# A two-layer hybrid encoder on one core: where the value products, the low halves and the gate products are issued

## The chip, the core and the metric

One core of a Trainium2 chip runs the whole program. TensorE (PE) multiplies, with its own queue for loading weights (PEld); VectorE (DVE), ScalarE (ACT) and GpSimd (POOL) work element by element; SyncE (SP) issues nearly all DMAs. The metric is the device time of one execution in microseconds; lower is better.

## The reference

Two layers over 512 tokens of a prompt and 256 of a sample, 1024 features, fp32. The same weights serve both.

```
h = rmsnorm(x, norm_mix_g);  proj = h @ w_in
qa, ka, va, qb, kb, vb, rb, glf, glb, ga, gb = split(proj)
ya = mixer_a(qa, ka, va) @ w_branch_a      # windowed softmax attention, 3 dilations x 8 heads
yb = mixer_b(qb, kb, vb, rb, ...) @ w_branch_b   # gated linear attention (GLA), both directions
x = x + (sigmoid(ga) * ya + sigmoid(gb) * yb) @ w_out
h = rmsnorm(x, norm_ffn_g)
x = x + relu(h @ w_ff1)**2 @ w_ff2
```

After the second layer comes one more rmsnorm. The changed code concerns the 1536 columns of `va`, taken in six blocks of 256 that are called values 0 to 5 (block 4 has the 32 low-rank columns `glf`, `glb` of the GLA decay beside it), the gates `ga` and `gb`, and the last stores.

## The kernel before, in words

Every fp32 product is made of three passes of a faster fp32 format: a factor is split into a high half (`whi`, `hh`, `sph`) by a cast on ACT and a low half (`wlo`, `hl`, `spl2`) by a subtraction on DVE or POOL, and hi x hi, hi x lo and lo x hi are added in PSUM. Dense products take their accumulators from a PSUM pool of three banks (`acc`): a fourth tile can start only when the first has been read out. A tile over the 1024 features is 8 x 3 = 24 matmuls.

The program is written as a stream of dense products beside steps of other work. `add` puts a product into the stream, `dense_piece` issues the next eighth or so of a tile, `weave(steps, total)` issues the steps with dense pieces spread evenly among them, up to `total` microseconds of an inner estimate, and `run_dense` issues what is left of the stream. The framework's scheduler then fixes each engine's order. An engine runs its own order strictly, and waits where an operand or a buffer is not ready.

A layer goes like this. **First stage**: `values(i, ...)` for three of six blocks: weights are loaded and split by `wunit` (`wlo` on the engine that `side[0]` names), six tiles of 128 tokens are multiplied, ACT and DVE split each result (`vst`) and SP stores it to `v_dram`; in between, the steps `lower` and `upper` (L1175 on) prepare operands of the Strassen form, normalised `xT`, their sums `t` and low halves `ql`, mostly on DVE. In layer 0 the prompt's tokens are loaded and their norm's statistics made in the middle of it (`statistics()`). **Projections** for queries and keys (`long_dense`). **Attention rounds**: one round before the first pair of heads, then `p` = 0, 1, 2, 3; PE, DVE and ACT work on scores, exponentials and outputs, and dense work is woven in as filler: the other values, gates `gate_a` and GLA values. **GLA heads**. **Gates and branches**: `gate_b(k)` multiplies two half-token tiles of 384 columns, which ACT evacuates into `sgb`; `split_from` loads the mixer's output from `ma_dram`, adds two parts on DVE, and splits the sum (`spl` on DVE, `sph` on ACT) into `xa`, which the product with `w_branch_a` reads. Then the product with `w_out`, the FFN, and in layer 1 `to_tokens`, which transposes the result and stores it in twelve DMAs.

Where the rows below say L235 they mean the matmuls of all ordinary dense products; L434 is a product of the projections, L173 the cast and L120 the subtraction of a split, L621 the gate's evacuation, L631 the cast in `split_from`, L626 its loads.

Of the kernel before, what the change touches and what calls it, by code (L numbers as in the profile page):

```python
# [24 lines left out]
NK = DM // 128  # L25
# [51 lines left out]
def encoder(ctx: ExitStack, tc: tile.TileContext, a, y_prompt, y_sample):  # L77
    nc = tc.nc
# [54 lines left out]
    def constants():  # L133
        nc.sync.dma_start(out=gmix[:, 1, :], in_=a["norm_mix_g"][1].rearrange("(k p) -> p k", p=128))
        for l in range(DEPTH):
            nc.sync.dma_start(out=gffn[:, l, :], in_=a["norm_ffn_g"][l].rearrange("(k p) -> p k", p=128))
        nc.sync.dma_start(out=qsc, in_=a["qscale"])
        nc.sync.dma_start(out=gfin, in_=a["final_norm_g"].rearrange("(k p) -> p k", p=128))
# [19 lines left out]
    ma_dram = drm.tile([2, 512, T], F32, name="ma_dram")  # L158
# [4 lines left out]
    side = [nc.gpsimd]  # L163
# [58 lines left out]
    def weave(steps, total):  # L222
        done = 0.0
        for i, step in enumerate(steps):
            step()
            while done < total * (i + 1) / len(steps):
                t = dense_piece()
                if t is None:
                    break
                done += t  # L230
# [392 lines left out]
    def split_from(drams, k, alloc_hi, alloc_lo):  # L623
        xs = [b3("spl") for _ in drams]
        for x, dram in zip(xs, drams):
            nc.sync.dma_start(out=x, in_=dram[k * 128:(k + 1) * 128, :])  # L626
        x = xs[0]
        for y in xs[1:]:
            nc.vector.tensor_tensor(x, x, y, op=ALU.add)
        hi, lo = alloc_hi("sph", F32R), alloc_lo("spl2", F32R)  # L630
        nc.scalar.copy(hi, x)  # L631
        sub(lo, x, hi)
        return hi, lo
# [398 lines left out]
    class Last:  # L1032
# [19 lines left out]

        def to_tokens(self, m):
            last = len(self.y) == NT and not any(self.left)
            if last:
                r = self.rms()
            for b in range(NT):
                if b not in self.y:
                    self.y[b] = b3("ya", shape=(128, 2, 384))
                y = self.y[b]  # L1060
                tp = pm("tp", (128, 2, 128))
                for i in range(2):
                    nc.tensor.transpose(tp[:, i, :], self.xT[m + 4 * i][:, b * 128:(b + 1) * 128], ident)
                if not last:
                    dst = y[:, :, m * 128:(m + 1) * 128]
                    nc.vector.tensor_copy(dst, tp) if (m + b) % 2 else nc.scalar.copy(dst, tp)
                    continue
                rb = r[:, b:b + 1]
                z = b3("yb", shape=(128, 2, 128))
                nc.scalar.activation(z, tp, AF.Copy, scale=rb)  # L1070
                nc.vector.tensor_scalar(y, y, rb, None, op0=ALU.mult)
                out, row = (y_prompt, b) if b < 4 else (y_sample, b - 4)
                out = out.rearrange("o s d -> (o s) d")[row * 128:(row + 1) * 128].rearrange("t (i c) -> t i c", i=2)
                nc.sync.dma_start(out=out[:, :, 0:384], in_=y)
                nc.sync.dma_start(out=out[:, :, 384:512], in_=z)

        def rms(self):
            sp = pm("st", (128, NT))
# [28 lines left out]
    def spill(k, xT):  # L1107
        nc.sync.dma_start(out=x_dram[k * 128:(k + 1) * 128, :], in_=xT[k])
# [4 lines left out]
    for l in range(DEPTH):  # L1113
        w_in = a["w_in"][l]
        nm = norm
        gxs = []
        side[0] = nc.gpsimd

        def values(i, low_rank, x, scaled, order=tuple(range(NT))):

# [34 lines left out]
            tok_dense(parts, nco, x, evac, order)  # L1155


        for i, low_rank in ((0, False), (4, True), (2, False)) if l == 0 else ((4, True), (2, False), (0, False)):
            values(i, low_rank, nm.h, True, (4, 5, 0, 1, 2, 3) if l == 0 else tuple(range(NT)))
        prefetch()  # L1160
        if l == 0:
            statistics = load_x(a["x_prompt"].rearrange("o s d -> (o s) d"), 0, SEQ, norm)
            for _ in range(2 * NK):
                dense_piece()
            statistics()
            for k in range(NK):
                spill(k, xT)
            constants()

        ops = Quads(4)  # L1170
# [13 lines left out]
        steps = [lambda: [nm.ready(t0, n) for t0, n in nm.parts]]  # L1184
# [10 lines left out]
            units.append([(c0 + hd * 128, R_GLA + 4 * i + hd, None if i else 128.0 ** -0.5, False)  # L1195
                          for i, c0 in enumerate((C_QB, C_KB))])
        long_dense(w_in, [(u[0][0], u[1][0]) for u in units], ops, projections([[c[1:] for c in u] for u in units]))
        weave(steps, 40 if l else 30)
        side[0] = nc.vector
        while len(stream) > 7 * len(units):  # L1200
            dense_piece()

# [48 lines left out]
        steps = [lambda b=b: gate_transpose(b) for b in range(NT)]  # L1251
# [49 lines left out]
            steps += [f] + nothing  # L1301
        steps += singles + [combine] + nothing * 4
        q, k, following = attention_load(1, x3)
        values(1, False, h_at, False)
        weave(steps + following, 14)
        run_dense()
        for p in range(4):
            steps = []
            if p < 3:
                scores, singles, combine, values1, loads, finish1 = attention_steps(p + 1, q, k)  # L1310
                extra = {4: scores[0], 6: scores[1], 8: scores[2], 15: loads[1]}
                extra.update({9 + i: f for i, f in enumerate(singles)})
                extra[11] = lambda f=extra[11], g=loads[0]: (f(), g())
            else:
                extra = {}
            for i, stages in enumerate(values_of):
                steps += stages
                if i in extra:
                    steps.append(extra[i])
            steps.append(finish)  # L1320
            if p < 3:
                steps += [combine] + nothing * 6
                values_of, finish = values1, finish1
            if p < 2:
                q, k, following = attention_load(p + 2, x3)
                steps += following
            if p == 0:
                values(3, False, h_at, False)
                values(5, False, h_at, False)
            elif p < 3:  # L1330
                for j in ((0, 1, 2), (3, 4))[p - 1]:
                    gate_a(j, True)
            else:
                gd = gla_dense(0, w_in, h_at, gn)
            weave(steps, (32, 23, 15, 32)[p])
            run_dense()

        def fetch_gates():
# [25 lines left out]
        def gate_b(k):  # L1364
            def evac(ci, t0, n, acc):
                if t0 == 0:
                    sgb.append(f3("sgb"))
                ins = gate(sgb[k][:, t0:t0 + n], acc[:, :n])
                if k == NK - 1 and t0:
                    with tc.issue_after(ins.ins if hasattr(ins, "ins") else ins):  # L1370
                        nc.scalar.preload_act_table_set("natural_log_exp_and_others")

            feat_dense(w_in, C_GB + k * 128, h_at, evac, splits=HALVES)

        xa = [split_from((ma_dram[0], ma_dram[1]), j, f3, f3) for j in range(4)]
        for j in range(4):
            gate_b(j)

        def evac(k, t0, n, acc):
            s = ta[k][:, t0:t0 + n]  # L1380
# [127 lines left out]
```

## Time and profile before

| | |
|---|---|
| runs | 3019.0, 3027.43, 3030.77 us, median 3027.43 |
| profiled execution | 3024.05 us, of which its span is 3022.2 us; mean granted clock 0.986 |
| PE | busy 2909.2 us, 96% |
| DVE | 2162.5 us, 72% |
| ACT | 1451.5 us, 48% |
| POOL | 64.7 us, 2% |

The span is from the first to the last instruction of the profiled execution. Busy time of engines overlaps, so the shares don't add up; an engine with 96% still hides stalls of some microseconds each and matmuls that run at half the clock.

### The profile page before, as it was taken

How to read it: one execution, taken by the hardware profiler on the slowest of the kernel's cores; microseconds unless marked ns; L12 is line 12 of the kernel's file. 1: busy time of each engine (PE TensorE's matmuls, PEld its weight loads, DVE VectorE, ACT ScalarE, POOL GpSimd, SP SyncE). 2: the span in 40 equal slices, each digit the busy share in tenths (PEclk: the TensorE clock that was granted, in tenths of full speed). 3: DMA queues.
4: the chain of work that ended last, by engine and by line, in shares of the span. 5: the costliest groups of instructions: out<-in, count | busy, mean ns of one | idle time of the engine just before them, and what ended most of it. 6: DMA issues, size and time to landing. Idle time of an engine off the chain costs nothing.

```text
span 3022.2 us, 49144 instructions
## 1 busy us (share of the span) xinstructions
PE 2909.2 (96%) x18428; PEld 2825.7 (93%) x18428; DVE 2162.5 (72%) x4594; ACT 1451.5 (48%) x3110; POOL 64.7 (2%) x128
## 2 busy tenths in 40 slices
PE   7999999999899999999999999899989999999997
PEld 7999988999799999999889999889988899999997
DVE  7767577887448777676986676778763587777767
ACT  5454677556234433333445547775552253333334
POOL 2000000000000000000010000000000000000000
PEclk9999999999999999999999999999999999999998
DMA  6345655233332222222234456643242231222212
GB/s 200 126 136 178 204 163 148 85 99 107 115 94 84 63 70 67 59 68 68 90 130 148 144 162 211 172 118 102 71 149 94 67 94 57 70 58 76 70 57 70
DMA packets 415070, 328.09 MB, mean 109 GB/s; under 512 B 44240, under 2 KB 369264, under 8 KB 414832
## 3 DMA queue, kind: packets, MB, share of 16 engines
q1 hardware_dynamic: 414832, 324.94, 35.3%
q8 instruction: 146, 2.39, 0.3%
q14 instruction: 92, 0.75, 0.1%
HBM read 248.44 MB, written 76.43 MB: 107 GB/s over the span
## 4 chain that ended last, share of the span: by engine, by line
PE 80%; DVE 8%; DMA 4%; ACT 3%; issue 1%; SPq 1%; POOL 0%; DVEq 0%; ACTq 0%
PE acc L235 41%; PE wA L434 11%; PE wA L360 8%; PE wC L434 5%; PE wC L360 4%; PE wB L434 3%; PE wB L360 2%; PE go L984 1%; DMA v_dram<-vst 1%; PE op L782 1%; DVE mt L799 1%; PE pt L770 1%; DVE xT L1462 1%; PE cp L906 1%; PE up L962 1%
## 5 line engine op out<-in xcount | busy, mean ns | idle before, releaser
L235 PE MATMUL acc<-hh,whi 128*128 128x384 f32 x1024 | 345.7, 338 | 0.0
L235 PE MATMUL acc<-hh,wlo 128*128 128x384 f32 x1024 | 344.2, 336 | 0.0
L235 PE MATMUL acc<-hl,whi 128*128 128x384 f32 x1024 | 343.7, 336 | 0.0
L173 ACT CAST whi<-raw 128x1024 fp32r<-128x1024 f32 (+1 forms) x176 | 185.2, 1053 | 291.7 <-PE acc L235 184.3
L120 DVE TENSOR_TENSOR wlo<-raw,whi 128x1024 fp32r<-128x1024 f32 x164 | 200.5, 1222 | 107.2 <-ACT whi L173 98.3
L434 PE MATMUL wA<-qh,aop 128*128 128x384 f32 x960 | 262.4, 339 | 4.3 <-ACT u L478 3.5
L1447 DVE SCALAR_TENSOR_TENSOR rl<-acc,nr 128x384 f32<-128x384 f32 x128 | 71.1, 555 | 190.6 <-PE acc L235 189.3
L235 PEld LDWEIGHTS acc<-hl,whi 128*128 128x128 f32 x1024 | 192.1, 188 | 0.9 <-DVE hl L549 0.4
L235 PEld LDWEIGHTS acc<-hh,whi 128*128 128x128 f32 x1024 | 192.2, 188 | 0.3
L235 PEld LDWEIGHTS acc<-hh,wlo 128*128 128x128 f32 x1024 | 192.2, 188 | 0.3
L434 PEld LDWEIGHTS wA<-qh,aop 128*128 128x128 f32 x960 | 176.8, 190 | 6.0 <-ACT u L478 4.1
L434 PE MATMUL wC<-qh,aop 128*128 128x384 f32 x640 | 178.3, 337 | 0.9 <-ACT aop L284 0.7
L434 PE MATMUL wA<-ql,aop 128*128 128x384 f32 x480 | 162.6, 339 | 0.0
L235 PE MATMUL acc<-whi,qh 128*128 128x256 f32 x528 | 155.2, 294 | 0.9 <-ACT whi L173 0.9
L235 PE MATMUL acc<-wlo,qh 128*128 128x256 f32 x528 | 151.5, 287 | 1.4 <-DVE wlo L120 1.4
L235 PE MATMUL acc<-whi,ql 128*128 128x256 f32 x528 | 150.6, 285 | 0.0
L1462 DVE TENSOR_TENSOR xT<-xT,wA 128x384 f32<-128x384 f32 x256 | 135.1, 548 | 16.6 <-PE wA L360 16.3
L284 ACT CAST sh<-s 128x512 fp32r<-128x512 f32 x128 | 78.1, 619 | 141.6 <-DVE s L334 100.6
L1448 ACT ACTIVATE hq<-rl 128x384 f32<-128x384 f32 x128 | 67.0, 524 | 153.5 <-DVE rl L1447 153.5
L284 ACT CAST aop<-raw 128x512 fp32r<-128x512 f32 x120 | 73.8, 619 | 120.4 <-PE wA L434 47.1
L235 PE MATMUL acc<-spl,whi 128*128 128x256 f32 (+1 forms) x384 | 129.9, 338 | 0.0
L284 ACT CAST aop<-wr 128x512 fp32r<-128x512 f32 x120 | 74.2, 619 | 115.6 <-PE wA L434 63.2
(355 smaller groups left out, 9109.5 us busy)
## 6 DMA issues: line engine op xcount, KB each, us to landing
raw<-in_w_in SPq DMA_DIRECT2D x88, 512.0 KB, 3.8
raw<-in_w_ff SPq DMA_DIRECT2D x64, 512.0 KB, 4.1
p_dram<-o SPq DMA_DIRECT2D x64, 384.0 KB, 2.3
v_dram<-vst SPq DMA_DIRECT2D x72, 256.0 KB, 2.2
raw<-in_w_in SPq DMA_DIRECT2D x64, 256.0 KB, 3.3
wr<-in_w_in SPq DMA_DIRECT2D x64, 256.0 KB, 4.6
raw<-in_w_ff SPq DMA_DIRECT2D x64, 256.0 KB, 3.4
raw<-in_w_ff SPq DMA_DIRECT2D x128, 128.0 KB, 2.8
```

The costliest lines, as they stand in the source:

```text
L120: eng.tensor_tensor(out, x, hi.bitcast(F32), op=ALU.subtract)
L173: nc.scalar.copy(hi, raw)
L235: nc.tensor.matmul(acc[:, :n], wt, xt, start=(k == 0 and j == 0), stop=(k == nkt - 1 and j == 2))
L284: nc.scalar.copy(hi, x)
L360: nc.tensor.matmul(acc[:, :HT], x, y, start=(new and p == 0 and j == 0), stop=(p == quads.n - 1 and j == 2), skip_group_check=True)
L434: nc.tensor.matmul(acc[:, :HT], x, y, start=(new and p == 0 and j == 0), stop=(p == n - 1 and j == 2), skip_group_check=True)
L770: nc.tensor.transpose(pt[:, g, hh, :], pr[hh][:, g * 128:(g + 1) * 128], ident)
L782: nc.tensor.matmul(op[:, hh], v[:, hh].rearrange("p s c -> p (s c)"), pT[g][:, hh].rearrange("p s c -> p (s c)"), start=(g == 0), stop=(g ...
L799: nc.vector.tensor_tensor(dst, dst, src, op=ALU.add)
L1447: nc.vector.scalar_tensor_tensor(r, acc[:, :n], 0.0, fnorm.r[:, t0:t0 + n], op0=ALU.max, op1=ALU.mult)
L1448: nc.scalar.activation(q[0][:, t0:t0 + n], r, AF.Square)
L1462: nc.vector.tensor_tensor(x, x, acc, op=ALU.add)
```

## The change

Four edits. (1) `values(1)` moves from the round before the first pair into the first stage; `values(3)` takes its place, `gate_a(0)` moves from round 1 to round 0 in place of `values(3)`, and the totals of the weaves follow. (2) POOL makes the low halves of weights only up to the prompt's statistics of layer 0; from then on DVE does. Before, POOL made them in the first stage of both layers. (3) The four products `gate_b(0)` to `gate_b(3)` are put into the stream, and 24 pieces of it issued, before the four `split_from` of `xa`. (4) The smaller one of each two last stores is issued from ACT's queue after the loop.

```diff
--- before.py
+++ after.py
@@ -1052,6 +1052,7 @@
 
         def to_tokens(self, m):
             last = len(self.y) == NT and not any(self.left)
+            stores = []
             if last:
                 r = self.rms()
             for b in range(NT):
@@ -1072,7 +1073,9 @@
                 out, row = (y_prompt, b) if b < 4 else (y_sample, b - 4)
                 out = out.rearrange("o s d -> (o s) d")[row * 128:(row + 1) * 128].rearrange("t (i c) -> t i c", i=2)
                 nc.sync.dma_start(out=out[:, :, 0:384], in_=y)
-                nc.sync.dma_start(out=out[:, :, 384:512], in_=z)
+                stores.append((out[:, :, 384:512], z))
+            for out, z in stores:
+                nc.scalar.dma_start(out=out, in_=z)
 
         def rms(self):
             sp = pm("st", (128, NT))
@@ -1114,7 +1117,6 @@
         w_in = a["w_in"][l]
         nm = norm
         gxs = []
-        side[0] = nc.gpsimd
 
         def values(i, low_rank, x, scaled, order=tuple(range(NT))):
 
@@ -1155,7 +1157,7 @@
             tok_dense(parts, nco, x, evac, order)
 
 
-        for i, low_rank in ((0, False), (4, True), (2, False)) if l == 0 else ((4, True), (2, False), (0, False)):
+        for i, low_rank in ((0, False), (4, True), (2, False), (1, False)) if l == 0 else ((4, True), (2, False), (0, False), (1, False)):
             values(i, low_rank, nm.h, True, (4, 5, 0, 1, 2, 3) if l == 0 else tuple(range(NT)))
         prefetch()
         if l == 0:
@@ -1165,6 +1167,7 @@
             statistics()
             for k in range(NK):
                 spill(k, xT)
+            side[0] = nc.vector
             constants()
 
         ops = Quads(4)
@@ -1195,8 +1198,7 @@
             units.append([(c0 + hd * 128, R_GLA + 4 * i + hd, None if i else 128.0 ** -0.5, False)
                           for i, c0 in enumerate((C_QB, C_KB))])
         long_dense(w_in, [(u[0][0], u[1][0]) for u in units], ops, projections([[c[1:] for c in u] for u in units]))
-        weave(steps, 40 if l else 30)
-        side[0] = nc.vector
+        weave(steps, 56 if l else 44)
         while len(stream) > 7 * len(units):
             dense_piece()
 
@@ -1301,7 +1303,7 @@
             steps += [f] + nothing
         steps += singles + [combine] + nothing * 4
         q, k, following = attention_load(1, x3)
-        values(1, False, h_at, False)
+        values(3, False, h_at, False)
         weave(steps + following, 14)
         run_dense()
         for p in range(4):
@@ -1325,14 +1327,14 @@
                 q, k, following = attention_load(p + 2, x3)
                 steps += following
             if p == 0:
-                values(3, False, h_at, False)
                 values(5, False, h_at, False)
+                gate_a(0, True)
             elif p < 3:
-                for j in ((0, 1, 2), (3, 4))[p - 1]:
+                for j in ((1, 2), (3, 4))[p - 1]:
                     gate_a(j, True)
             else:
                 gd = gla_dense(0, w_in, h_at, gn)
-            weave(steps, (32, 23, 15, 32)[p])
+            weave(steps, (23, 15, 15, 32)[p])
             run_dense()
 
         def fetch_gates():
@@ -1372,9 +1374,11 @@
 
             feat_dense(w_in, C_GB + k * 128, h_at, evac, splits=HALVES)
 
-        xa = [split_from((ma_dram[0], ma_dram[1]), j, f3, f3) for j in range(4)]
         for j in range(4):
             gate_b(j)
+        for _ in range(3 * NK):
+            dense_piece()
+        xa = [split_from((ma_dram[0], ma_dram[1]), j, f3, f3) for j in range(4)]
 
         def evac(k, t0, n, acc):
             s = ta[k][:, t0:t0 + n]
```

ACT's order in layer 0 around the gates; `whi` is the high half of a gate's weights, `mbt` the end of the GLA part, `sph` the four casts of `split_from`, `sgb` the gates' evacuations. Before:

```order
L1017 COPY mbt_9081<-tp_9650 128x256
L1017 COPY mbt_9081<-tp_9671 128x256
L1017 COPY mbt_9081<-tp_9681 128x256
L631 CAST sph_9713<-spl_9708 128x768
L631 CAST sph_9722<-spl_9717 128x768
L631 CAST sph_9731<-spl_9726 128x768
L631 CAST sph_9740<-spl_9735 128x768
L621 ACTIVATE sgb_9781<-acc_9756 128x384
L621 ACTIVATE sgb_9781<-acc_9783 128x384
L621 ACTIVATE sgb_9840<-acc_9815 128x384
L173 CAST whi_9929<-raw_9927 128x1024
L621 ACTIVATE sgb_9840<-acc_9842 128x384
```

After:

```order
L621 ACTIVATE sgb_9745<-acc_9720 128x384
L1017 COPY mbt_9081<-tp_9671 128x256
L1017 COPY mbt_9081<-tp_9681 128x256
L621 ACTIVATE sgb_9745<-acc_9747 128x384
L621 ACTIVATE sgb_9804<-acc_9779 128x384
L631 CAST sph_9811<-spl_9806 128x768
L173 CAST whi_9929<-raw_9927 128x1024
L621 ACTIVATE sgb_9804<-acc_9842 128x384
L631 CAST sph_9820<-spl_9815 128x768
L631 CAST sph_9829<-spl_9824 128x768
L631 CAST sph_9838<-spl_9833 128x768
L621 ACTIVATE sgb_9899<-acc_9874 128x384
```

Three evacuations moved ahead of the first cast, a fourth between the first and the second, and the fifth stands behind the fourth cast.

POOL's order from the start of the program's weights on (its `wlo` of layer 0, then the zeroing of attention buffers); before:

```order
L120 TENSOR_TENSOR wlo_203<-raw_200,whi_202 128x1024
L120 TENSOR_TENSOR wlo_209<-raw_206,whi_208 128x1024
L120 TENSOR_TENSOR wlo_296<-raw_292,whi_295 128x1152
L120 TENSOR_TENSOR wlo_559<-raw_555,whi_558 128x1152
L120 TENSOR_TENSOR wlo_565<-raw_562,whi_564 128x1024
L120 TENSOR_TENSOR wlo_847<-raw_844,whi_846 128x1024
L663 MEMSET qk_3157 64x768
```

After:

```order
L120 TENSOR_TENSOR wlo_203<-raw_200,whi_202 128x1024
L120 TENSOR_TENSOR wlo_209<-raw_206,whi_208 128x1024
L120 TENSOR_TENSOR wlo_296<-raw_292,whi_295 128x1152
L663 MEMSET qk_3333 64x768
L663 MEMSET qk_3334 64x768
```

DVE's order in the first stage of layer 0, after the change, where two of these three subtractions now stand (behind line 1055 the changed file's line numbers are up to four higher):

```order
L318 TENSOR_TENSOR t24_528<-xT_104,t24_528 128x384
L1140 SCALAR_TENSOR_TENSOR vst_548<-acc_504,rt_180,vst_548 128x4x64
L120 TENSOR_TENSOR wlo_556<-raw_552,whi_555 128x1152
L120 TENSOR_TENSOR ql_542<-t24_528,qh_541 128x768
L120 TENSOR_TENSOR wlo_562<-raw_559,whi_561 128x1024
L1155 CAST gx_594<-eye_79 128x2
L1140 SCALAR_TENSOR_TENSOR vst_590<-acc_565,rt_180,vst_590 128x4x64
L1150 TENSOR_SCALAR gl_595<-acc_565,rt_180 128x32
```

The subtractions `wlo_556` and `wlo_562` stand between the low halves of the Strassen operands, ahead of evacuations `vst`; POOL keeps three of its six in layer 0, and none of the six in layer 1.

SP's last stores before (`ya` is the larger piece, `yb` the smaller):

```order
L1075 DMA y_prompt<-yb_32853 256x1x128
L1074 DMA y_prompt<-ya_32557 256x1x384
L1074 DMA y_prompt<-ya_32562 256x1x384
L1075 DMA y_prompt<-yb_32861 256x1x128
L1074 DMA y_prompt<-ya_32567 256x1x384
L1075 DMA y_prompt<-yb_32869 256x1x128
L1074 DMA y_prompt<-ya_32572 256x1x384
L1075 DMA y_prompt<-yb_32877 256x1x128
```

ACT's end after the change (SP keeps the six `ya`):

```order
L1071 ACTIVATE yb_32881<-tp_32878,fr_32841 128x256
L1071 ACTIVATE yb_32888<-tp_32885,fr_32841 128x256
L1078 DMA y_prompt<-yb_32853 256x1x128
L1078 DMA y_prompt<-yb_32860 256x1x128
L1078 DMA y_prompt<-yb_32867 256x1x128
L1078 DMA y_prompt<-yb_32874 256x1x128
L1078 DMA y_sample<-yb_32881 256x1x128
L1078 DMA y_sample<-yb_32888 256x1x128
```

The six `yb` stores left SP's queue and stand behind the last activation of ACT.

## Rows read from the trace of the kernel before

**Rows 1.** The page's first part: busy time of each engine, its share of the span, and its number of instructions.

```profile
PE 2909.2 (96%) x18428; PEld 2825.7 (93%) x18428; DVE 2162.5 (72%) x4594; ACT 1451.5 (48%) x3110; POOL 64.7 (2%) x128
```

**Rows 2.** PE's waits over the whole span: instruction that waited, what released it, then us in total, times, longest us.

```profile
PE acc L235 <- ACT sgb L621: 26.6, 2, 14.3
...
PE acc L235 <- POOL wlo L120: 4.9, 3, 2.8
```

**Rows 3.** The timeline of PE where the gate products of layer 0, and below them those of layer 1, pass into the next tile. Columns: start us, duration us, engine, line, operation, out<-in, partitions x elements; in brackets the idle time before and what released it. A matmul's end is modelled; its pace is read from start to start.

```profile
764.14 0.33 PE L235 MATMUL acc<-ql,whi 128*128 128x384 f32 x1
...
765.36 0.34 PE L235 MATMUL acc<-qh,wlo 128*128 128x384 f32 x1
777.97 0.69 PE L235 MATMUL acc<-b12h,whi 128*128 128x384 f32 x1 [12.27 <-ACT sgb L621]
...
2255.73 0.34 PE L235 MATMUL acc<-qh,wlo 128*128 128x384 f32 x1
2270.38 0.69 PE L235 MATMUL acc<-b12h,whi 128*128 128x384 f32 x1 [14.32 <-ACT sgb L621]
```

**Rows 4.** PE in the 4 us behind the first of these two waits and in the 18 us after them. Columns: stretch, its length, PE's busy time and matmuls, granted clock (1.00 is 2.4 GHz, 0.50 is 1.2 GHz), DMA share, GB/s.

```profile
778.00:782.00 4.00, 4.00 (x13) 0.50 0.01 4
782.00:800.00 18.00, 18.00 (x102) 0.97 0.28 98
```

**Rows 5.** The timeline of the other engines in layer 0 up to the end of that wait (SPq is SP's queue of DMA issues).

```profile
762.43 1.22 DVE L120 TENSOR_TENSOR wlo<-raw,whi 128x1024 fp32r<-128x1024 f32 x1
...
763.41 3.95 SPq L626 DMA_DIRECT2D spl<-ma_dram  x7
...
767.19 0.96 DVE L629 TENSOR_TENSOR spl<-spl 128x768 f32<-128x768 f32 x1 [3.54 <-DMA spl<-ma_dram]
...
768.18 0.83 ACT L631 CAST sph<-spl 128x768 fp32r<-128x768 f32 x1 [5.26 <-DVE spl L629]
...
776.70 0.83 ACT L631 CAST sph<-spl 128x768 fp32r<-128x768 f32 x1 [1.89 <-DVE spl L629]
777.43 1.25 ACT L621 ACTIVATE sgb<-acc 128x384 f32<-128x384 f32 x3
```

**Rows 6.** The attention rounds 0, 1 and 2 of layer 0, then of layer 1, cut where SP loads the next pair's `l_dram` (the engines' order is PE, PEld, DVE, ACT, POOL; a bracket holds the number of instructions).

```profile
367.00:422.20 55.20, 52.24 (x439) 50.83 (x438) 40.31 (x135) 41.58 (x126) 3.48 (x13) 0.97 0.62 190
422.20:468.20 46.00, 43.54 (x306) 41.12 (x307) 34.88 (x124) 34.42 (x114) 3.93 (x14) 1.00 0.66 178
468.20:515.40 47.20, 42.56 (x289) 37.71 (x287) 37.19 (x127) 38.23 (x119) 2.39 (x12) 1.00 0.47 128
1852.00:1910.00 58.00, 52.49 (x440) 51.08 (x439) 40.97 (x135) 42.22 (x128) 3.49 (x13) 0.97 0.59 180
1910.00:1958.00 48.00, 45.12 (x306) 42.66 (x307) 34.98 (x124) 34.65 (x114) 3.93 (x14) 0.96 0.65 171
1958.00:2005.40 47.40, 42.46 (x289) 37.56 (x287) 37.14 (x127) 38.29 (x118) 2.39 (x12) 1.00 0.47 125
```

**Rows 7.** The timeline of PE at two value matmuls of 256 columns in layer 0 and at the first projection product behind the values; then at two of 288 columns in layer 1 and at the first projection product there.

```profile
39.00 0.28 PE L235 MATMUL acc<-whi,hl 128*128 128x256 f32 x1
39.12 0.28 PE L235 MATMUL acc<-wlo,hh 128*128 128x256 f32 x1
...
89.20 0.52 PE L434 MATMUL wA<-b11h,aop 128*128 128x384 f32 x2
...
1533.00 0.29 PE L235 MATMUL acc<-whi,hl 128*128 128x288 f32 x1
1533.13 0.29 PE L235 MATMUL acc<-wlo,hh 128*128 128x288 f32 x1
...
1578.30 0.34 PE L434 MATMUL wA<-b11h,aop 128*128 128x384 f32 x1
```

**Rows 8.** The matmuls into `acc` from 38 to 92 us, grouped by operands (three groups of the same size, the first shown): duration min/median/max in ns, first and last start, forms with their counts.

```profile
L235 PE MATMUL acc<-whi,hh x104: 278/295/685, 38.1 to 88.8; 128*128 128x256 f32 x56, 128*128 128x288 f32 x48
```

**Rows 9.** All engines while the value products run, layer 0 and layer 1 (columns as in the rounds).

```profile
38.00:89.20 51.20, 44.63 (x323) 43.52 (x321) 45.65 (x86) 23.03 (x42) 10.20 (x3) 0.93 0.39 127
1533.00:1578.30 45.30, 40.17 (x315) 39.13 (x314) 42.65 (x71) 22.34 (x38) 8.37 (x3) 0.96 0.42 140
```

**Rows 10.** The timeline of DVE there: the first and the last of nine instructions that take longer than their equals, and an equal.

```profile
43.94 2.98 DVE L120 TENSOR_TENSOR ql<-xT,qh 128x768 fp32r<-128x768 f32 x1
...
49.50 0.95 DVE L120 TENSOR_TENSOR ql<-t,qh 128x768 fp32r<-128x768 f32 x1
...
1560.11 3.08 DVE L120 TENSOR_TENSOR ql<-t,qh 128x768 fp32r<-128x768 f32 x1
```

**Rows 11.** The timeline of POOL: two subtractions in layer 0 and one in layer 1.

```profile
41.32 7.84 POOL L120 TENSOR_TENSOR wlo<-raw,whi 128x1152 fp32r<-128x1152 f32 x2 [20.50 <-ACT whi L173]
...
1499.07 2.69 POOL L120 TENSOR_TENSOR wlo<-raw,whi 128x1152 fp32r<-128x1152 f32 x1 [993.35 <-ACT whi L173]
```

**Rows 12.** The timeline of PE in the value products of layer 0.

```profile
46.17 0.61 PE L235 MATMUL acc<-wlo,hh 128*128 128x288 f32 x1 [2.75 <-POOL wlo L120]
```

**Rows 13.** All engines at the program's end (the last three columns: granted clock, DMA share, GB/s).

```profile
3012.00:3021.00 9.00, 0.00 (x0) 0.00 (x0) 0.69 (x2) 0.00 (x0) 0.00 (x0) 0.50 0.95 333
```

**Rows 14.** The timeline of SP's queue there, first and last row.

```profile
3009.98 0.62 SPq L1075 DMA_DIRECT2D y_prompt<-yb  x1
...
3018.26 0.58 SPq L1075 DMA_DIRECT2D y_sample<-yb  x1
```

## The prediction

> **What bounds the kernel now.** The page's first part [rows 1] says that TensorE (PE) is busy for 96% of 3022.2 us, with no other engine over 72%. So nothing that only lightens VectorE (DVE), ScalarE (ACT) or GpSimd (POOL) counts by its busy time; what counts is PE's idle time, PE's slow clock, and PE work that can move to where PE would otherwise stand still. I went on to PE's waits [rows 2]: the largest is two waits on the gate evacuation `sgb`, 26.6 us together. After that I read the stages that the change touches: PE's own rows at those two waits [rows 3, 4], the other engines there [rows 5], the attention rounds between which work is moved [rows 6], the first stage that receives it [rows 7 to 9], the subtractions on POOL [rows 10 to 12] and the last stores [rows 13, 14].
>
> **Gates ahead of the splits.** In layer 0 PE starts the last product of a gate tile at 765.36 and the next tile only at 777.97; in layer 1 it is 2255.73 and 2270.38 [rows 3]. Less the 0.17 us that a matmul takes from start to start (seven in the 1.22 us from 764.14 to 765.36), the idle times are 12.4 and 14.5 us. The rows of the other engines say why [rows 5]. SP issues the loads of `spl` from 763.41, DVE adds the first pair at 767.19 after a wait for them, ACT casts the first `sph` at 768.18 and the fourth at 776.70, and the `sgb` evacuations stand behind these casts in ACT's order: they run at 777.43, three in a row. Three accumulators are all that this pool has, so PE had nowhere to write. The weights were not what it lacked: the low half of the next gate's was made at 762.43. After the wait the clock was at its lower level: 13 matmuls in the 4.00 us from 778.00 at a granted clock of 0.50, against 102 in 18.00 us right behind it at 0.97 [rows 4]. Thirteen at the later pace are 2.3 us, so 1.7 us more is lost in each layer (the first row after the wait in layer 1 has the same 0.69 us). In all 12.4 + 14.5 + 2 x 1.7 = 30.3 us.
>
> In the changed order of ACT three evacuations stand ahead of the first `sph`, the next behind one cast alone, and the fifth behind the fourth cast. A tile is 24 matmuls of 0.174 us, 4.2 us: the fourth to the seventh tile would run from about 765 to 782. The evacuation behind one cast can start when that cast ends, near 769.0 by the present times, where its bank is wanted at about 778; the fifth near 777.5, wanted at about 782. The splits then end where they do now, near 778, and `branch_a`, which reads them, comes 14 us of gate products later than before. I take the whole -30.3. The bound on the other side: should the new order leave the fifth and sixth evacuation late, half of it stays (-15).
>
> **Values moved into the first stage.** A value product is six tiles of 24 matmuls at 0.119 us (39.00 to 39.12 in [rows 7]), 17.2 us of PE; with the 288 columns of the low-rank one they come at 0.133. In layer 0 the value tiles run from 38.1 [rows 8] to 89.20, 51.1 us; what they consist of is 168 matmuls of 256 columns and 144 of 288 [rows 8], 168 x 0.119 + 144 x 0.133 = 39.2 us. So 11.9 us are not value work, while DVE is busy for 45.65 of 51.20 [rows 9]. If the added product filled all of that, the stage would grow by 17.2 - 11.9 = 5.3 us; if none, by 17.2. One hole comes before any weight of the new product can be there: PE's 2.75 us at 46.17 [rows 12]. I take 5.3 + 2.75 = +8.0. In layer 1 the stretch from 1533.0 to 1578.3 (45.3 us) holds 24 matmuls of 288 columns and 288 of 256, 37.5 us; 7.8 are free, the growth is between 17.2 - 7.8 = 9.4 and 17.2, and I take +9.4, since the added product becomes a queue with which DVE no longer sets the pace: its 42.65 us there [rows 9] plus two low halves and six evacuations (2 x 1.22 [rows 5] and about 6 x 0.5) are 48, against 37.5 + 17.2 = 54.7 of PE. Sum: +17.4, at worst +34.4.
>
> **The rounds that lose work.** The round before the first pair swaps one value product for another and stays. Round 0 has two value products beside the attention (34.4 us), after the change one and a gate: 17.2 + 48 x 0.174 = 25.6. Round 1 has three gates, 25.1 us, after it two, 16.7, which is what round 2 has now and keeps. So each round's new filler is that of a round that is in the trace [rows 6]: round 0 took 55.2 and 58.0 us, round 1 46.0 and 48.0, round 2 47.2 and 47.4. That round 2 with a third less filler is no shorter than round 1 is the main point: below some 46 to 47 us a round goes by its own chain on ACT, DVE and PE (ACT is busy for 38.2 of 47.2 us there, more than in round 1). Round 0 comes down to its successor's time, -9.2 and -10.0; round 1 changes to round 2's, +1.2 and -0.6. Sum: -18.6. If PE's work paid in full it would be two times -17.2 = -34.4; if round 1 grew by 1.2 in both and round 0 gained only what PE loses there (34.4 - 25.6 = 8.8), it would be -15.2.
>
> **Low halves from POOL to DVE.** Three of them move in layer 0 and six in layer 1. While POOL subtracts, a DVE instruction is held: `ql` at 43.94 takes 2.98 us where the same takes 0.95 at 49.50, and at 1560.11 3.08 [rows 10] beside a POOL row like the one at 41.32, two subtractions in 7.84 us [rows 11]. Nine such DVE rows, the first and last shown, are longer than their equals by 16.1 us; about 14 of it belongs to the nine that move. In return DVE gets nine subtractions of 1.22 us [rows 5], 11.0. DVE wins some 3 us while PE, with its longer queue, sets the pace: I count 0. The cover is the value product in the first stage; without it the 3 us would be a gain. The Trainium skill, in "SBUF — State Buffer", section "SBUF: two separate sides", says that a POOL instruction and a DVE instruction with two SBUF inputs exclude each other for the whole instruction; the held rows agree in kind. By that rule DVE could be held for all of POOL's time, an estimated 9 x 2.7 us, and would win 10 us more; the time would be the same by both, as DVE is hidden.
>
> **Last stores.** Six stores leave SP's queue for ACT's. SP's stores are issued from 3009.98 to 3018.26 [rows 14], 8.3 us for twelve; from two queues it could be about half. But from 3012 to 3021 the DMA engines are 95% busy at 333 GB/s [rows 13]: 3 MB have to be written, and an earlier issue only makes the queue longer. The 5% that are free of those 9 us are 0.5, so the bounds are 0 and -0.5; I take 0. Here the change does what it says and its time does not move. The Trainium skill, "DMA: Bandwidth & Descriptors", section "Issuing engines are not separate DMA queues", says that all issuers end on the same engines and that only issue time is saved; with that alone as much as 4 us would be hoped for, where the row leaves next to nothing.
>
> **Sum.** 3024.05 (the profiled execution: span 3022.2 and 1.85 around it) - 30.3 + 17.4 - 18.6 + 0 + 0 = 2992.6. The median of the runs is 3.4 above that execution: 2996.
>
> **Rivals.**
> A. PE work pays in full in the rounds (-34.4 for -18.6): 2980. For it: PE is busy for 42.5 of 47 us even in round 2, as full as elsewhere. Against it: round 2 is no shorter than round 1.
> B. The first stage grows by all of the moved work, because its holes are waits for DVE and for weights, and more PE work doesn't reach them: +34.4 for +17.4, 3013. For it: DVE's 89% and 94% there, and four weight casts more on ACT. Against it: ACT is busy for half of these stretches, and the added tiles' operands are the same `hh` and `hl` that are already there.
> C. Half of the gate wait comes back behind the casts: 3011.
> D. Slower: the low halves now queue behind DVE's operands, and PE waits for them. Thirteen are concerned, the nine moved and the four of the two added value products. If each cost what PE lost at 46.17 to one from POOL, 2.75 us [rows 12], it would be +35.7: 3032. It decides from (3027.4 - 2996) / 13 = 2.4 us for each. For it: DVE's 89% and 94% there. Against it: one takes 1.22 us instead of POOL's 2.7 to 3.9 [rows 11], and only 3 waits of PE on one show now, 4.9 us [rows 2].
>
> **Chances.** The forecast 0.60, A 0.15, B 0.13, C 0.08, D 0.04. A measurement of this kernel can tell about 0.5% from no change, 15 us. The forecast and A are faster by more; B at 3013 and C at 3011 lie at that bound and go about half to each side; D is within it, or slower if its waits are longer: faster 0.84, same 0.14, slower 0.02. The range reaches from A to B: 2980 to 3013.
>
> **What would show it.** Right: no wait on `sgb` of over 3 us, and no 0.50 clock before `branch_a`; value tiles of layer 0 ending near 97 and of layer 1 near 1588 less what layer 0 gained; round 0 at 46 to 48 us and round 1 unchanged; no DVE row of 3 us among 0.95s after the prompt's statistics; the stores ending some 11 us after the first of them is issued, as now. Wrong: a round 0 that stays above 52 us, a first stage 17 us longer, or PE waits on `wlo` in the value tiles.

## The result and the profile after

The changed kernel takes 2974.83 us, the median of four runs (2974.24 to 2976.52), beside 3027.02 for the kernel before. The ratio is 0.9832, with a 95% interval of 0.9812 to 0.9852: 52 us faster, where 31 were forecast. The direction was right and the time lies 5 us below the range of 2980 to 3013.

The first part of the page of the changed kernel, against [rows 1]:

```profile
PE 2901.2 (98%) x18428; PEld 2813.7 (95%) x18428; DVE 2152.8 (72%) x4603; ACT 1448.7 (49%) x3110; POOL 38.4 (1%) x119
```

PE has the same 18428 matmuls in a span that is 49.5 us shorter (2972.7 us). Its mean granted clock went from 0.986 to 0.996. The difference is time in which PE stood still or ran at the lower clock.

PE's waits in the changed kernel, the longest first, with the one on POOL that is left (columns as in [rows 2]):

```profile
PE pt L770 <- ACT t L764: 6.5, 6, 2.0
...
PE acc L235 <- POOL wlo L120: 1.2, 1, 1.2
```

No wait on `sgb` is left anywhere in the list, and the waits on POOL's `wlo` are down from 4.9 to 1.2. The next three views show the places that the prediction named. First ACT's timeline at the gates of layer 0, the counterpart of [rows 5]:

```profile
756.59 0.50 ACT L621 ACTIVATE sgb<-acc 128x384 f32<-128x384 f32 x1
...
757.49 0.54 ACT L621 ACTIVATE sgb<-acc 128x384 f32<-128x384 f32 x1
760.17 0.49 ACT L621 ACTIVATE sgb<-acc 128x384 f32<-128x384 f32 x1 [2.14 <-PE acc L235]
762.00 0.83 ACT L631 CAST sph<-spl 128x768 fp32r<-128x768 f32 x1 [1.34 <-DVE spl L629]
...
765.11 0.48 ACT L621 ACTIVATE sgb<-acc 128x384 f32<-128x384 f32 x1
...
771.02 0.83 ACT L631 CAST sph<-spl 128x768 fp32r<-128x768 f32 x1 [1.89 <-DVE spl L629]
771.76 0.49 ACT L621 ACTIVATE sgb<-acc 128x384 f32<-128x384 f32 x1
```

Three evacuations run ahead of the first cast; the third one waits for PE, no longer PE for it. Then all engines in the 30 us around that place, and after it in the two first stages (from 38 us, and from the first low-rank transpose of layer 1, to the first projection product; columns as in [rows 6]):

```profile
756.00:786.00 30.00, 30.00 (x174) 29.28 (x173) 16.45 (x20) 12.92 (x21) 0.00 (x0) 1.00 0.64 226
...
38.00:97.50 59.50, 58.00 (x462) 57.30 (x463) 49.21 (x99) 28.63 (x51) 0.00 (x0) 1.00 0.49 158
1513.00:1563.70 50.70, 50.70 (x425) 50.70 (x424) 40.53 (x71) 23.09 (x40) 0.00 (x0) 1.00 0.52 169
```

PE is busy throughout, but for 1.5 us in the first stage of layer 0, at the full clock. In [rows 9] PE had 44.63 of 51.20 and 40.17 of 45.30 us in these stages (in layer 1 from the value tiles at 1533, 3.4 us behind the first low-rank transpose), with granted clocks of 0.93 and 0.96. Where the holes were filled, the clock came back too.

To see where the 52 us come from, I cut each layer at three instructions that every kernel has: the last product of the projections (L434), the last of the GLA heads (L984), and the first `sgb` evacuation. The columns are the lengths between them in the profiled executions, in us. The pieces of layer 1 begin at the last w_out product of layer 0.

| kernel | L0: start to projections | L0: rounds, GLA | L0: to gates | L1: to projections | L1: rounds, GLA | L1: to gates |
|---|---|---|---|---|---|---|
| before | 335.1 | 418.2 | 24.1 | 827.0 | 422.5 | 25.3 |
| after | 342.5 | 405.3 | 8.8 | 830.9 | 405.4 | 8.8 |
| one_gates | 334.3 | 418.3 | 8.8 | 825.7 | 422.6 | 8.8 |
| one_side | 334.9 | 423.0 | 24.7 | 820.6 | 425.0 | 24.3 |
| one_values | 347.4 | 405.6 | 24.1 | 841.0 | 407.2 | 24.5 |
| after_pool | 348.6 | 406.2 | 8.8 | 843.6 | 405.6 | 8.8 |
| idle_pool | 341.1 | 423.5 | 24.8 | 836.5 | 422.8 | 24.0 |
| gate0_round1 | 342.7 | 406.3 | 8.8 | 832.6 | 405.2 | 8.8 |
| five_values | 357.7 | 390.9 | 8.8 | 850.8 | 391.3 | 8.8 |

Kernels whose rounds are identical (before, one_gates, one_side, idle_pool) differ by up to 5 us in one profiled execution: that is what a single figure here is good for. The profiled execution of one_gates is 5 us below the median of its runs, that of one_side 7 above. Before to after: gates -15.3 and -16.5, first stages +7.4 and +3.9, rounds with GLA heads -12.9 and -17.1, together -50.5.

### The profile page after: what moved, and what is told of

It is laid out like the page before. It is cut to its first block, busy times and chain, and to the rows that moved or that the text cites. A ratio compares the mean times of both kernels' runs of the same rounds, so it can differ in the third digit from the quotient of the medians.

```text
span 2972.7 us, 49103 instructions
## 1 busy us (share of the span) xinstructions
PE 2901.2 (98%) x18428; PEld 2813.7 (95%) x18428; DVE 2152.8 (72%) x4603; ACT 1448.7 (49%) x3110; POOL 38.4 (1%) x119
## 4 chain that ended last, share of the span: by engine, by line
PE 84%; DVE 7%; ACT 3%; DMA 3%; issue 1%; SPq 1%; POOL 0%; DVEq 0%; ACTq 0%
PE acc L235 44%; PE wA L434 11%; PE wA L360 8%; PE wC L434 5%; PE wC L360 4%; PE wB L434 3%; PE wB L360 2%; PE go L984 1%; DVE mt L799 1%; PE sp L745 1%; DMA qkx<-p_dram 1%; PE op L782 1%; PE cp L906 1%; PE up L962 1%; PE ap L944 1%
## 5 line engine op out<-in xcount | busy, mean ns | idle before, releaser
L120 DVE TENSOR_TENSOR wlo<-raw,whi 128x1024 fp32r<-128x1024 f32 (+1 forms) x173 | 211.7, 1224 | 78.8 <-ACT whi L173 69.7
L434 PE MATMUL wA<-qh,aop 128*128 128x384 f32 x960 | 261.0, 338 | 4.4 <-ACT u L478 3.3
L434 PEld LDWEIGHTS wA<-qh,aop 128*128 128x128 f32 x960 | 176.0, 189 | 6.0 <-ACT u L478 3.8
L434 PE MATMUL wC<-qh,aop 128*128 128x384 f32 x640 | 177.5, 336 | 0.0
L434 PE MATMUL wA<-ql,aop 128*128 128x384 f32 x480 | 161.8, 337 | 0.0
L1466 DVE TENSOR_TENSOR xT<-xT,wA 128x384 f32<-128x384 f32 x256 | 134.9, 547 | 16.8 <-PE wA L360 16.5
L235 PE MATMUL acc<-whi,qh 128*128 128x256 f32 x480 | 140.9, 294 | 0.2
L235 PE MATMUL acc<-wlo,qh 128*128 128x256 f32 x480 | 137.8, 287 | 1.5 <-DVE wlo L120 1.5
L235 PE MATMUL acc<-whi,ql 128*128 128x256 f32 x480 | 136.5, 284 | 0.0
```

Source lines behind the costliest of these rows:

```text
L120: eng.tensor_tensor(out, x, hi.bitcast(F32), op=ALU.subtract)
L235: nc.tensor.matmul(acc[:, :n], wt, xt, start=(k == 0 and j == 0), stop=(k == nkt - 1 and j == 2))
L434: nc.tensor.matmul(acc[:, :HT], x, y, start=(new and p == 0 and j == 0), stop=(p == n - 1 and j == 2), skip_group_check=True)
L1466: nc.vector.tensor_tensor(x, x, acc, op=ALU.add)
```

## The experiments

### Each edit alone

The expectations below speak of two theories that the result suggested. R: the rounds give back nearly all the PE work taken from them, and POOL's subtractions cost nothing. P: POOL's subtractions hold up the first stage. The four edits, each put on the kernel before by itself: of the diff, the hunk with `range(3 * NK)` for one_gates; all lines on `values`, `gate_a` and the weaves for one_values; the lines on `side[0]` for one_side; `to_tokens` for one_stores.

> The kernel before with the gate edit alone (24 pieces of the gate products issued ahead of the four splits). Both theories: the two waits on sgb go and nothing takes their place, -30 to -32 us, 2995 to 2997. If half of the wait returned behind the casts, -15.

> The kernel before with the moved value product, the moved gate and the totals of the weaves alone; POOL still makes the low halves. Theory R (the rounds give back nearly all of the PE work taken from them, about 30 us where 18.6 were expected, and POOL's subtractions cost nothing): about -18 us, 3009. Theory P (the subtractions on POOL hold up the first stage, so the added product fills less of it while they stay there): -6 to -10 us, and the first stages grow by 20 us and more. Theory of the prediction: -1.

> The kernel before with the low halves moved from POOL to DVE behind the prompt's statistics, alone. Theory R: 0, within 3 us. Theory P: -8 to -12 us, since in the first stage as it was DVE sets the pace and wins 3 us, and PE no longer waits for a POOL subtraction of 2.4 to 3.9 us. The prediction said that without the added product the 3 us that DVE wins would be a gain: -3.

> The kernel before with the six smaller last stores on ACT's queue, alone. All theories: 0, within 1 us; the DMA engines are 95% busy while the stores are written. If the issue time of SP's queue bound the end, -3 to -4 us.

Measured, beside a median of 3027.78 for the kernel before:

| | median us | ratio, 95% interval | against before |
|---|---|---|---|
| one_gates | 2994.99 | 0.9890 (0.9876 to 0.9904) | -32.8 |
| one_values | 3022.38 | 0.9983 (0.9974 to 0.9992) | -5.4 |
| one_side | 3017.57 | 0.9966 (0.9954 to 0.9977) | -10.2 |
| one_stores | 3028.35 | 0.9996 (0.9987 to 1.0005) | +0.6 |

The sum is -47.8 of the -52. The gates and the stores are what both theories and the prediction said. The moved values alone gain 5.4 us, a little less than the 6 to 10 of theory P and far from the 18 of R; the low halves gain 10.2 without any work being taken away, as P said. The table of stages shows why the values gain so little by themselves: with POOL still subtracting, the first stages grow by 12.3 and 14.0 us, against 7.4 and 3.9 in the changed kernel, while the rounds give nearly the same (-12.6 and -15.3 against -12.9 and -17.1).

### What about the low halves costs time

one_side says that moving them off POOL helps, not by what. Either PE waits for a result that POOL makes late (2.4 to 4.8 us for one, where DVE needs 1.2 to 1.4), or DVE is held while POOL subtracts. The kernel before shows both kinds of wait: beside the 4.9 us on POOL's `wlo` in [rows 2], PE waits for an accumulator that DVE reads out into `gl`:

```profile
PE acc L235 <- DVE gl L1148: 6.7, 3, 3.3
```

To see whether the hold alone costs time, DVE makes the low halves and POOL does the same subtraction again, into a buffer that nobody reads (the hunks that switch `idle[0]` are left out here):

```diff
         sub(lo, raw, hi, side[0])
+        if idle[0]:                    # where one_side has moved the subtraction
+            sub(raw, raw, hi, nc.gpsimd)
```

> The low halves on DVE as in one_side, and behind each of the nine moved ones POOL makes the same subtraction a second time, into the dead weight buffer, for nobody. Theory W (what cost 10 us was PE waiting for a result that POOL makes late): the gain of one_side stays, 3017 to 3020. Theory H (what cost was DVE, held while POOL subtracts): the gain goes, and as DVE now has the nine subtractions beside the holds, the time is that of the kernel before or up to 10 us above it, 3027 to 3038.

Measured: 3041.38 us, ratio 1.0045 (1.0033 to 1.0058): 13.1 us slower than before and 23.8 slower than one_side, from nine subtractions whose results nobody reads (only the next load into that buffer waits for them, as it does in the kernel before). Theory W, that waits for POOL's results were all that cost, falls. Theory H had the direction, and its range ended 3 us too low. DVE and POOL in the first stage of layer 0 of idle_pool, while POOL's idle subtraction runs:

```profile
49.03 7.51 POOL L120 TENSOR_TENSOR raw<-raw,whi 128x1152 f32<-128x1152 f32 x2 [27.07 <-DVE wlo L120]
...
49.59 1.21 DVE L120 TENSOR_TENSOR wlo<-raw,whi 128x1024 fp32r<-128x1024 f32 x1
50.73 2.66 DVE L1156 CAST gx<-eye 128x2 fp32r<-128x2 f32 x1
```

And the same copy of two columns in one_side:

```profile
50.45 0.16 DVE L1152 CAST gx<-eye 128x2 fp32r<-128x2 f32 x1
```

A copy of 0.16 us takes 2.66, so it isn't work but a hold. It ends at 53.39, just as the first of the two subtractions in POOL's row does (from 49.03, 4.34 us long). The hold goes both ways: DVE's own subtraction just before took its usual 1.21 us, and POOL's took 4.34 where the same size at 19.30 took 2.66. In the whole stage, one_side first and idle_pool below, DVE's busy time grows by 6 us:

```profile
38.00:89.70 51.70, 43.13 (x317) 41.38 (x316) 44.01 (x90) 24.01 (x42) 0.00 (x0) 0.97 0.40 131
...
38.00:94.70 56.70, 46.06 (x317) 44.06 (x318) 50.02 (x91) 24.22 (x43) 10.41 (x3) 0.91 0.37 120
```

The same 317 instructions of PE take 5 us more, 2 of them idle and 3 at a lower clock. PE's waits on what DVE reads out of an accumulator, over the whole span, idle_pool first:

```profile
PE acc L238 <- DVE vst L1141: 7.1, 4, 2.8
...
PE acc L238 <- DVE gl L1151: 5.8, 4, 1.8
...
PE acc L238 <- DVE gx L1156: 5.1, 3, 3.9
...
PE acc L235 <- DVE gx L1152: 6.2, 4, 3.9
...
PE acc L235 <- DVE gl L1147: 2.3, 2, 1.7
...
PE acc L235 <- DVE vst L1137: 1.5, 1, 1.5
```

When DVE is held, the bank stays full and PE waits: 18.0 us for the three in idle_pool, 10.0 in one_side, where POOL subtracts nothing behind the statistics. A rival, that POOL's reading of the buffer delays the next weights, hardly shows: PE's waits on `whi` are 2.2 us against 2.0. The hold agrees with the rule of the Trainium skill ("SBUF — State Buffer", section "SBUF: two separate sides") that was weighed in the prediction, by which the two exclude each other for a whole instruction. The section names DVE instructions with two SBUF inputs or in a mode that uses both ports; the copy has one input, and no row shows its mode.

The counterpart undoes that edit in the changed kernel, so that POOL subtracts beside the longer queue of PE:

```diff
-            side[0] = nc.vector        # behind the statistics of layer 0
+        side[0] = nc.vector            # behind the weave, in both layers
```

> The changed kernel with the low halves of the first stages left on POOL. If the effects of the four edits, taken alone, add up: 3027.8 - 32.8 - 5.4 + 0.6 = 2990. If the low halves cost nothing, as predicted: 2975. In the profile, theory H wants the first stages of both layers longer than in the changed kernel by 5 and 10 us, with PE's waits there ended by DVE's vst, gl and gx.

Measured: 2991.89 us, ratio 0.9881 (0.9867 to 0.9894), 17 us above the changed kernel (16, each against its own runs of the kernel before) and within 2 of the sum of the effects alone. With the added product in place the low halves are worth 16 to 17 us, so they were not hidden by it. But here 13 subtractions change place, nine and the four of the added products: 1.2 to 1.3 us each, where one_side has 1.1. The first stage of layer 0 of after_pool, as the windows of the changed kernel above, and below it the longest of all PE's waits in that kernel:

```profile
38.00:102.70 64.70, 60.04 (x461) 58.80 (x461) 52.60 (x94) 28.27 (x51) 15.51 (x5) 0.97 0.44 145
...
PE acc L235 <- POOL wlo L120: 7.3, 7, 3.0
```

The window has 461 matmuls, as the changed kernel's has 462, in 64.7 us instead of 59.5, at a clock of 0.97 instead of 1.00; DVE's busy time is 3.4 us more although it has five subtractions fewer. The stages are longer than the changed kernel's by 6.1 and 12.7 us, as expected. The expected sign is not there in layer 0: PE's idle time is a wait for POOL's `wlo` (4.7 us in this window), not for `vst`, `gl` or `gx`; in layer 1 it waits 2.9 us for `gx` and `gl` and 1.5 for POOL. Both causes are thus at work, the hold of DVE and POOL's late results, and no run separates their shares in the 16 to 17 us.

### Whether PE work pays in the rounds

The other large miss is the rounds. Two kernels move or drop one gate, `gate_a(0)`, 48 matmuls in each layer (no_gate0 then reads gate 1 in its place; that hunk is left out here):

```diff
 # gate0_round1, from the changed kernel
-                gate_a(0, True)
-                for j in ((1, 2), (3, 4))[p - 1]:
+                for j in ((0, 1, 2), (3, 4))[p - 1]:
-            weave(steps, (23, 15, 15, 32)[p])
+            weave(steps, (16, 23, 15, 32)[p])
 # no_gate0, from the kernel before
-                for j in ((0, 1, 2), (3, 4))[p - 1]:
+                for j in ((1, 2), (3, 4))[p - 1]:
-            weave(steps, (32, 23, 15, 32)[p])
+            weave(steps, (32, 15, 15, 32)[p])
```

> The changed kernel with gate_a(0) back in round 1 (round 0 keeps values(5) alone, round 1 has three gates as before the change). Theory F (PE's work pays in full in every round): 0 to 1 us, 2975, since it is the same work. Theory C (round 0 is bound by PE and pays more than its work, rounds 1 and 2 go by their own chain and take a gate for nothing): round 0 shorter by 8 us, rounds 1 and 2 longer by 0 to 3, in both layers, -10 to -16 us, 2959 to 2965.

> The kernel before with gate_a(0) left out of round 1 and gate 1 used in its place (part of the computation is left out): 48 matmuls, 8.4 us of PE in each layer, with their weights, casts and stores. Theory F: -16.7 us, 3011. Theory C: rounds 1 and 2 as long as they were, 0 to -4 us, 3024 to 3028.

Measured: gate0_round1 2977.13 us (ratio 0.9831, 0.9818 to 0.9845, which is the changed kernel's), no_gate0 3010.95 (0.9944, 0.9930 to 0.9957). Moving the gate from round 0 to round 1 changes nothing; leaving it out gains 17.3 us where its matmuls are 16.7. Both are what theory F said, and theory C, the one that the prediction was built on, is wrong: over the whole kernel a gate is not free. Where the 17.3 us are saved no trace shows: in no_gate0's profiled execution, 5 us above its median, the rounds and GLA heads are 0.2 us longer than before in layer 0 and 6.3 shorter in layer 1.

### Is there more to be had

Two kernels go further along the same way. One gives DVE the three low halves that POOL still makes; the other moves `values(3)` into the first stage as well (`(3, False)` joins its list, in a hunk that is left out here, and the rounds' weaves follow with 15, 8, 15, 32):

```diff
-    side = [nc.gpsimd]                            # all_dve
+    side = [nc.vector]
-        weave(steps, 56 if l else 44)                 # five_values
+        weave(steps, 72 if l else 58)
-        values(3, False, h_at, False)                 # before round 0; now in the first stage
+        values(5, False, h_at, False)
-                values(5, False, h_at, False)
                 gate_a(0, True)
+                gate_a(1, True)
-                for j in ((1, 2), (3, 4))[p - 1]:
+                for j in ((2,), (3, 4))[p - 1]:
```

> The changed kernel with the three low halves that POOL still makes in layer 0 on DVE too. Theory H: one of the three falls into the stretch in which DVE prepares the operands, where it holds an instruction for 2 us; 0 to -3 us against the changed kernel, 2972 to 2975. If DVE had no room left, slower: 2977 and more.

> The changed kernel with values(3) in the first stage too (values(5) before round 0, gates 0 and 1 in round 0, gate 2 alone in round 1). Theory F with a first stage whose holes are filled: the rounds lose 34.4 us of PE work and that much time, the first stages grow by 30 to 34, 0 to -4 us: 2971 to 2975. If the first stages still had room, as they had for the first of the two, -15 and more; if the rounds now went by their own chain, slower than 2985.

Measured: all_dve 2977.84 us (0.9838, 0.9823 to 0.9852), 3 us above the changed kernel and not to be told from it, five_values 2982.52 (0.9851, 0.9835 to 0.9867), 8 above. The expectation for all_dve rested on a wrong row: the three low halves that POOL still makes in the changed kernel run from 10.88 to 21.4 us, ahead of the stretch in which DVE prepares the operands, so nothing was held there to be won. The second says that there were holes for one product, not for two. All engines in the first stage of layer 0 of five_values:

```profile
38.00:113.00 75.00, 75.00 (x607) 74.46 (x605) 54.06 (x106) 33.23 (x58) 0.00 (x0) 1.00 0.49 160
```

PE is busy for all 75 us: the stage grows by 15.2 us in layer 0 and 19.9 in layer 1 over the changed kernel, and the rounds give 14.4 and 14.1 back, less than the 17.2 us of matmuls moved. No kernel tried beats the changed one.

## Why the prediction was wrong where it was wrong

**Gates: right.** -30.3 forecast, -32.8 measured alone. The idle time and the slow clock behind it, as summed, account for it within the interval. The new evacuation behind the fourth cast, the one that the bound of -15 was for, runs at 771.76, and the window from 756 to 786 has PE busy without a gap.

**Low halves: a term put at 0 that measured -10.2 alone and 16 to 17 us with the added product.** The prediction balanced DVE's instructions (some 14 us of holds removed, 11 us of subtractions added, so 3 won) and then called DVE hidden, because PE's longer queue would set the pace. Two steps failed. The balance counts DVE's own time, but a hold also costs what waits behind DVE: in idle_pool nine idle subtractions cost 23.8 us, with longer waits of PE and a lower clock (0.91 for 0.97). And PE's waits for POOL's results, 4.9 us in [rows 2], stayed out of the sum. One of them, the 2.75 us at 46.17 [rows 12], was even kept as a hole that the added product can't fill, although edit 2 moves that very subtraction to DVE. The added subtractions did not show: with them DVE is busy for 49.21 of 59.50 us, and PE's idle time is 1.5. Nor did the long queue hide POOL's subtractions. With them (after_pool) the first stages grow by 13.5 and 16.6 us, near rival B's 17.2 each; without, by 7.4 and 3.9. In layer 1 the holes were also counted from 1533 only, while three of the six subtractions, the first at 1499.07 [rows 11], run before that.

**First stages: near in the sum, for a partly wrong reason.** +17.4 forecast, +11.3 in the profiled executions. Against one_side, which has the low halves on DVE and not the product, the growth is 7.6 and 10.3, 17.9. So the term for the product comes out as computed, from stages that another edit had made faster, in layer 1 at least (one_side: -0.2 and -6.4).

**Rounds: the step that failed.** -18.6 forecast, -30.0 measured. The step is "each round's new filler is that of a round that is in the trace", and with it that round 0 comes down to its successor's time and that the round before the first pair stays. I cut the rounds where SP loads the next `l_dram`, took the filler of each from the code, and concluded from 46.0 us with 25.1 of filler and 47.2 with 16.7 that rounds go by a chain of their own. The filler is not that of the code. PE's matmuls of dense products in rounds 1 and 2 of layer 0, the kernel before above and the changed kernel below (PE busy, number, clock, DMA):

```profile
422.20:468.20 46.00, 30.44 (x138) 1.00 0.66 178
468.20:515.40 47.20, 24.56 (x121) 1.00 0.47 128
...
418.40:468.00 49.60, 25.26 (x119) 1.00 0.56 159
468.00:511.20 43.20, 22.39 (x112) 1.00 0.48 128
```

Before, round 1 has 138 gate matmuls, some 24 us; round 2 has 121, some 19 us in all, since 29 of them are smaller ones of the GLA values that the code gives to the next round. The gap is 5 us, not 8.4, because dense products run ahead of the cut. The rows on which I based the step already showed it: rounds 1 and 2 of [rows 6] have 306 and 289 matmuls, 17 apart, where two gate tiles would have made 48. That explains a part only. With 5 us more of filler round 1 is still no longer than round 2 in layer 0, and in the changed kernel, with 3 us more, it is 6.4 longer. The lengths by these cuts, before and after, in us:

| | layer 0 | layer 1 | change | forecast |
|---|---|---|---|---|
| before the first pair | 31.9, 23.7 | 29.9, 22.6 | -8.2, -7.3 | 0 |
| round 0 | 55.2, 52.2 | 58.0, 52.9 | -3.0, -5.1 | -9.2, -10.0 |
| round 1 | 46.0, 49.6 | 48.0, 48.6 | +3.6, +0.6 | +1.2, -0.6 |
| round 2 | 47.2, 43.2 | 47.4, 43.4 | -4.0, -4.0 | 0 |

The remaining -1.3 in each layer lies behind round 2. Of the -30.0, -15.5 before the first pair and -8.0 in round 2 lie where nothing was forecast, and round 0 stays above 52 us, the prediction's own sign of being wrong. The cuts don't hold the same work in both kernels (PE has 242 instructions before the first pair, and 211 after the change), a single round by them does not follow its filler, and what sets its length stays open. What the runs show is the sum: of the 34.4 us of matmuls moved out, 30.0 came back here, 27.9 in one_values, and 28.5 of the next 34.4 in five_values. So rival A had nearly the right rule (PE work pays in full: -34.4) and was given 0.15; I argued against it with the misread rows.

**Stores: right.** +0.6, within the interval of no change, alone. The last 9 us of transfers in the changed kernel, against [rows 13] (last columns: clock, DMA share, GB/s), and SP's first store, against [rows 14]:

```profile
2963.00:2972.00 9.00, 0.00 (x0) 0.00 (x0) 0.04 (x1) 0.00 (x0) 0.00 (x0) 0.50 0.89 302
...
2960.48 3.57 SPq L1075 DMA_DIRECT2D y_prompt<-ya  x4
```

With two issuers the DMA engines are 89% busy, against 95% with one, and from the first store's issue to the end of the span it is 12.2 us in both kernels.

**Sum.** Between the two profiled executions the forecast was -31.5 us and the spans differ by -49.5. Of the 18 us missed, 11.4 are the rounds, 6.1 the first stages (product and low halves together) and 1.5 the gates; 1 us has the other sign. The medians lie 3 us further apart than the profiled executions do. Rival A had the rounds' miss, and no rival had that of the low halves, so the range ended at 2980. Rival D (thirteen low halves late on DVE) had no part: PE's waits on `wlo`, from POOL and DVE together, went from 6.3 to 2.7 us.

## What to carry to other kernels

Before a stretch is compared with another by length, count in the trace the matmuls that each holds: a row of code isn't a measure, since the scheduler moves filler over the cut, and here a count of evacuations isn't one either (both rounds have five `sga` evacuations for 24 and 19 us of filler). Where PE is 90% busy, take filler as paid for nearly in full (30.0 of 34.4 us here) unless an experiment leaves it out for nothing. An instruction of a neighbour engine that stretches DVE's cost here what waited behind DVE, PE and its clock included, not DVE's balance of busy time. When two edits meet in one stage, look whether one removes the hole that the other is to fill.

## What the runs showed of the hardware that was not expected

A POOL subtraction with both inputs in SBUF holds even a DVE copy of two columns: 2.66 us for 0.16. Nine such subtractions that nothing depends on made the kernel 23.8 us slower, 2.6 us each, where one takes 2.35 to 4.34 us on POOL in that kernel. And the first stages came back to a granted clock of 1.00 from 0.93 and 0.96 when their holes were filled.
